# A two-layer transformer with experts: layer 1's first modulation product moved into layer 0's routing, and the split weights' tiles lent to the first experts

## The chip, the cores and the metric

The kernel runs on one core of one Trainium2 chip. The metric is the device time of one execution in microseconds. Before the change it is 1314.4 us, the median of 3 runs (1313.9 to 1314.6). The core has TensorE (PE, and PEld for its weight loads), VectorE (DVE), ScalarE (ACT), GpSimd (POOL) and SyncE (SP); SP is used here to issue the loads of weights, ACT and POOL issue other transfers. A "q" behind an engine's name (SPq) is its queue of transfers.

## What is computed

Two layers of a diffusion transformer work on 256 latent tokens and 256 context tokens of width 1024, in float32. In each layer a vector per stream, silu(c), is multiplied by `w_ada` (1024 x 6144) and gives six modulation vectors. The tokens, scaled and shifted by the first two of these, go through a mixer: differential attention with 4 heads, a depthwise convolution of 31 taps, sigmoid gates and an output projection. A layer norm with residual follows, then a mixture of 16 experts: a router picks 2 experts for each token, each expert is `(silu(h w_gate) * (h w_up)) w_down` with inner width 512, and another layer norm with residual ends the layer. Cut to what matters:

```
mod   = split(silu(c) @ w_ada[l] + b_ada[l], 6)
h     = x * (1 + mod[1]) + mod[0]
x     = layer_norm(ALPHA * x + mod[2] * mixer(h), ln1_g[l], ln1_b[l])
h     = x * (1 + mod[4]) + mod[3]
x     = layer_norm(ALPHA * x + mod[5] * grouped_moe(h), ln2_g[l], ln2_b[l])
```

In the last layer only the latent tokens are carried on.

## The kernel before, in words

**Modulation** (`ada`, L339). The 6144 columns of `w_ada` are done in three groups of 2048. A group takes 8 loads of 1 MB (128 rows each, L347) and, for each load, one group of matmuls: four products with 32 rows of output, side by side on TensorE (L349; the profile shows two records for each product, so 8 for a load). The sum stands in one PSUM bank through all 8 loads. Then the bias is added, which two small transfers on POOL brought (L345), the row is transposed, and two DVE copies write `modT`. `ada` is a generator that yields after each load, so that other code can run it a few loads at a time.

**Weights.** Nearly all weights come through `load_raw` (L240), one SP transfer of 1 MB into a tile of 128 x 2048. The usual tiles are the `raw` ring of 3. Products of many tokens use a three-term split: ACT casts the weights to float32r (`whi`, L258), DVE takes the rest (`wlo`, L259), each into rings of 4 tiles of 128 x 1024, and `mm3` (L289 to L293) multiplies high by high, and high by low twice. Where few tokens meet an expert, `raw` is multiplied directly in float32 (`expert64`, L1235 and L1256; `expert32`, L1281 and L1301).

**Layer 0's mixer** (L465). Weights of blocks of 512 columns are multiplied one after the other, and a hook `fill` (L1533) is called between. Its first ten calls run two loads each of `ada(0, 1)` and `ada(0, 2)`, the other two groups of layer 0; the later calls, from the attention on, run two loads each of `ada(1, 0)`, layer 1's first group. So this product's loads and matmuls lie in layer 0's attention, beside the gates' products. The attention of each head is a chain over TensorE (scores, L625), DVE (maximum, L630), ACT (exponential, L632), DVE, transposes, ACT and TensorE again (L646). After the mixer, six small DVE operations (L1551 to L1553) combine layer 1's `modT` with layer 0's last norm into the scale and shift `gt`, `bt` that layer 1's mixer begins with.

**Output projection and routing.** `out_proj` (L751) multiplies by `w_out`, normalizes, computes the router's logits and writes the modulated tokens to DRAM (`hdr`, L866). `route` (L870) is mostly small DVE operations on 128 partitions, with two short groups on TensorE (L942 and L944, L972). It gives an order of the experts by number of tokens (`rank`, `erow`) and the indices `gidx`, `sidx`, `idx2` of the tokens. POOL then gathers the tokens of the first tasks with indirect transfers (`fetch`, L1107).

**Experts of layer 0.** They run in the order of L132, by rank: 0, 1, 8, 9, 10, 2, 3, ... Ranks 0 and 1 are always experts 14 and 15 (`AHEAD`, L96), so their weights can be asked for before the routing is known; for each later one SP reads the expert's number first (L1404). An expert takes 6 loads of 1 MB. Ranks 0, 1 and 8 to 15 have few tokens and use `raw` weights directly; ranks 2 to 7 split them. `loads` (L1069) is lazy, and the steps of consecutive experts are interleaved (L1412), so the loads come in the order gate, gate, up, up of the first expert, gate, gate, up, up of the second, down, down of the first, and so on. The tiles come from `most_tiles` (L211), which goes round through the 3 `raw` tiles, 4 tiles of its own (`raw2`, named raw in the profile) and the two large tiles `m0a`, `m0b`: 9 in all.

**What sets the order.** The code names the engine of each operation. The order on each engine and queue is made by the framework when the kernel is built, from the order in the code, the dependences and a simulated timeline (L1596); `follow` (L249) adds order edges by hand. On the chip each engine and each queue works through its list strictly in order, and an instruction that waits holds all behind it.

Of the kernel before, what the change touches and what calls it, by code (L numbers as in the profile page):

```python
# [24 lines left out]
F32 = mybir.dt.float32  # L25
F32R = mybir.dt.float32r
# [117 lines left out]
N2 = (4, 3)  # L144
# [7 lines left out]
def dit_kernel(ctx: ExitStack, tc: tile.TileContext, A, out):  # L152
    nc = tc.nc
    V, S, G, PE, SP = nc.vector, nc.scalar, nc.gpsimd, nc.tensor, nc.sync
# [3 lines left out]
    ring = ctx.enter_context(tc.tile_pool(name="ring", bufs=1))  # L158
    pm = ctx.enter_context(tc.tile_pool(name="pm", bufs=1))
# [5 lines left out]
    def bank(tag):  # L165
        pool, cfg = banks["now"]
        return pool.tile([128, 512], F32, name=tag, bufs=cfg[tag])

    class scoped:


        def __init__(self, name, keep=False, **cfg):
            assert sum(cfg.values()) <= 8
            self.sb = tc.tile_pool(name=name, bufs=1, reuse_waits="tile")
            self.ps = None if keep else tc.tile_pool(name=name + "_ps", bufs=1, space=bass.MemoryType.PSUM, reuse_waits="tile")
            self.cfg = cfg
# [23 lines left out]
    def raw_tile():  # L200
        return ring.tile([128, 2048], F32, name="raw", bufs=3)

    def more_tiles(pool):

        while True:
            for i in range(pool[1]):
                if i < 3:
                    yield raw_tile()
                yield own_tile(pool)

    def most_tiles(pool, extra):  # L211

        while True:
            for i in range(pool[1]):
                if i < 3:
                    yield raw_tile()
                yield own_tile(pool)
            for name in ("m0a", "m0b"):
                yield pm.tile([128, 2048], F32, name=name)
            if extra:  # L220
                yield pm.tile([128, 2048], F32, name="m1a")

    def own_tile(pool):
        return pool[0].tile([128, 2048], F32, name="raw2", bufs=pool[1])

    def own_tiles(pool):
        while True:
            yield own_tile(pool)

    raws = {"from": None}  # L230
# [8 lines left out]

    def load_raw(src, pat=None, after=None, **kw):  # L240
        t = next(raws["from"]) if raws["from"] else raw_tile()
        hold["load"] = SP.dma_start(t.rearrange(pat, **kw) if pat else t, src)
        if after is not None or hold["y"] is not None:
            follow(hold["load"], after or hold["y"])
        return t
# [3 lines left out]
    def follow(inst, other):  # L249

        tc.add_manual_dep(getattr(inst, "ins", inst), getattr(other, "ins", other).name, in_order,
                          reason="off the critical path")
        return inst

    hold = {"split": None, "y": None}
# [19 lines left out]
    def block_raws(w3, c0, nk, after=None):  # L275

        return [load_raw(w3[:, k0:k0 + 4, c0:c0 + 512], "p (k n) -> p k n", after, n=512) for k0 in range(0, nk, 4)]
# [17 lines left out]
    def transposed(ps, src, n=128):  # L295
        return PE.transpose(ps, src, ident[:src.shape[0], :src.shape[0]])
# [42 lines left out]
    def ada(l, g, tag):  # L339

        ps = bank(tag)
        bv = bias.rearrange("(j q) n -> j q n", q=32)
        src = A["b_ada"][l, g * 2048:(g + 1) * 2048].rearrange("(j n) -> j n", j=4)
        for i in range(2):
            G.dma_start(bv[:, i, :], src)  # L345
        for k in range(KC):
            raw = load_raw(A["w_ada"][l, k * 128:(k + 1) * 128, g * 2048:(g + 1) * 2048])  # L347
            for j in range(4):
                PE.matmul(ps[32 * j:32 * j + 32, :], cs[:, k, :], raw[:, j * 512:(j + 1) * 512],  # L349
                          start=k == 0, stop=k == KC - 1, tile_position=(0, 32 * j))  # L350
            if k < KC - 1:
                yield
        m = small.tile([128, 512], F32, name="modrow", bufs=1)
        V.tensor_tensor(m, ps, bias, op=OP.add)
        if g == 0:
            ps = bank("tr")
            for c in range(4):
                transposed(ps[:, c * 128:(c + 1) * 128], m[:, c * 128:(c + 1) * 128])
            pv = ps.rearrange("p (c j s) -> p c j s", c=4, j=4)
            V.tensor_copy(modT[l][:, :, 0:2, :], pv[:, :, 0:2, 0:2])  # L360
            V.tensor_scalar(modT[l][:, :, 2:4, :], pv[:, :, 2:4, 0:2], 1.0, None, op0=OP.add)
        else:
            dst = moddr[l][:, g * 2048:(g + 1) * 2048].rearrange("s (j n) -> s j n", j=4)
            mv = m.rearrange("(j q) n -> j q n", q=32)
            for i in range(2):
                G.dma_start(dst[i], mv[:, i, :])
        yield

    def run(steps, n=None):
        while n is None or n > 0:  # L370
            if next(steps, 0) == 0:
                return
            n = None if n is None else n - 1
# [88 lines left out]
    def first_block(l):  # L462
        return block_parts(block_raws(A["w_in"][l].rearrange("(k p) n -> p k n", p=128), U_OFF + CC, KC), (V, V) if l else (G, G))
# [605 lines left out]
    def loads(l, e, rows=False):  # L1069
        for src, n in units(l, e, rows):  # L1070
            yield load_raw(src, "p (k n) -> p k n", n=n)
# [5 lines left out]
    def chunks(raws, n, engs=((V, V), (V, V))):  # L1077
        res = []
        for e in engs:
            for hi, lo in split_unit(next(raws), e):  # L1080
                for j in range(0, 1024, n):
                    res.append((hi[:, j:j + n], lo[:, j:j + n]))
        return res

    def first_gate(l, pre):
        raws["from"] = more_tiles(pre)
        ws = loads(l, DENSE[l], True)
        return ws, chunks(ws, 512, ((V, V), (G, G)))

    def moe(l, lg, mh, ml, xn, early, pre_cm, pre):  # L1090
        last = l == NL - 1
# [22 lines left out]
        def more(tasks):  # L1114

            while len(ahead) < len(tasks):
                ts = tasks[:len(ahead) + 1]
                if sum(t[1] for t in ts if not isinstance(t, int)) > 3 or sum(isinstance(t, int) for t in ts) > 3:
                    return
                ahead.append(fetch(ts[-1]))  # L1120
# [261 lines left out]
        order = expert_order(l)  # L1382
        ahead.append(fetch(order[0]))
        more(order)

        for tt in range(T // 128):
            for h in range(4):
# [2 lines left out]
                hold["x1"] = G.tensor_tensor(xn[tt][:, hs], xn[tt][:, hs], res[1][:, hs], op=OP.add)  # L1390
        if DENSE[l] is not None:
            dense(*early, [([mh[k // 4][:, k % 4, tt] for k in range(KC)], [ml[tt][:, k] for k in range(KC)]) for tt in range(T // 128)])
        raws["from"] = most_tiles(pre, last)
        before = iter(())
        for n, task in enumerate(order):
            more(order[n:])
# [4 lines left out]
            if rk < len(AHEAD[l]):  # L1401
                src = loads(l, AHEAD[l][rk])
            else:
                src = loads(l, SP.value_load(erow[0:1, rk:rk + 1], min_val=0, max_val=NE - 1))  # L1404
            if rk in TINY[l]:
                steps = expert32(src, *xs, TINY[l].index(rk))
            elif isinstance(task, int):
                steps = expert64(src, *xs, FEW[l].index(rk))
            else:
                steps = expert(src, xs, [CAP[l] * rk + i for i in range(task[1])])  # L1410
# [9 lines left out]
        first = None if last else first_block(l + 1)  # L1420
# [85 lines left out]
    for tt in range(4):  # L1506
        src = (A["x"] if tt < 2 else A["ctx"])[0, (tt % 2) * 128:(tt % 2) * 128 + 128, :]
# [14 lines left out]
    def ahead():  # L1522
        yield from ada(0, 1, "po")
        yield from ada(0, 2, "sc")
        scaled_rows(0)

    def later():
        yield from ada(1, 0, "mm")

    steps, calls = ahead(), [0]  # L1530
    steps2 = later()

    def fill():  # L1533
        calls[0] += 1
        t = calls[0]
        if t <= 10:
            run(steps, 2 if t > 1 else 0)
        else:
            run(steps2, 2)

    m = mixer(0, xT, lambda k, s: modT[0][:, k % 4, 2 + k // 4, s:s + 1],
              lambda k, s: modT[0][:, k % 4, k // 4, s:s + 1], fill)
    gt = cst.tile([128, KC, 2], F32, name="gt1")
    bt = cst.tile([128, KC, 2], F32, name="bt1")
    pt0 = prm[0][0]
    for s in range(2):
# [4 lines left out]
        V.tensor_tensor(gv, scv, pt0[:, 13:21].rearrange("p (j c) -> p j c", j=2), op=OP.mult)  # L1551
        V.tensor_tensor(bv, scv, pt0[:, 21:29].rearrange("p (j c) -> p j c", j=2), op=OP.mult)
        V.tensor_tensor(bv, bv, shv, op=OP.add)  # L1553

    def experts(l, m, res_src):
        pre_cm = scoped(f"pre{l}", True)
        pre = (pre_cm.open(), N2[l])
        lg, early, xn = out_proj(l, *m, res_src, lambda: first_gate(l, pre))
        return moe(l, lg, *m[:2], xn, early, pre_cm, pre), xn

    first, x1 = experts(0, m, res0)

    def ahead():
        yield from ada(1, 1, "po")
# [3 lines left out]
    steps = ahead()  # L1568
    ticks = iter((1,) * 4 + (2,) * 6)

    def fill1():
        run(steps, next(ticks, 16))

    m = mixer(1, None, lambda k, s: gt[:, k, s:s + 1], lambda k, s: bt[:, k, s:s + 1], fill1,
              lambda s, pool, modulate: combine(0, s, x1, pool, modulate), first)
    _, x1 = experts(1, m, lambda tt: xres[tt * 128:tt * 128 + 128, :])
# [23 lines left out]
```

## Time and profile before

| what | value |
|---|---|
| median of 3 runs | 1314.4 us (1313.9 to 1314.6) |
| the profiled execution: its time, its span | 1314.02 us, 1312.2 us |
| mean granted TensorE clock over the span | 0.927 of full speed |
| PE busy | 1119.2 us (85%) |
| DVE busy | 757.6 us (58%) |
| ACT busy | 451.9 us (34%) |
| POOL busy | 265.4 us (20%) |
| SP's transfer queue (q1) | 304.11 MB, 60.2% of 16 engines' span |
| HBM read and written over the span | 262 GB/s |

Times in the rows below are microseconds from the start of the span. Busy time is the time in which an engine had an instruction running; matmuls overlap, so a TensorE that is busy all the time need not be at its peak. In the order of time a line gives start, duration, engine, source line, operation, output and inputs, and how many were merged; what stands in brackets is the idle time before it and who ended that. [...]

### The profile page before, as it was taken

Reading aid. Unit: us, or ns where it says so; the run is one execution under the profiler, and the core shown is the slowest. Engines: PE = TensorE matmul, PEld = TensorE weight load, DVE = VectorE, ACT = ScalarE, POOL = GpSimd, SP = SyncE. Lnnn points to the kernel's source line nnn. Section 1 sums busy time; section 2 is a strip of 40 time slices with the busy share of each in tenths; the row PEclk is TensorE's granted clock in tenths of the full one; section 3 lists DMA queues with packets and bytes.
Section 4 is the critical chain, followed back from the end, with each engine's and each line's share of the span. In section 5 each row is a group of like instructions: output and inputs, shape, how many; then the busy total and the mean of one; then the engine's idle time right before and its main releaser. Section 6 shows DMA issues by size and latency. Waiting matters only on the chain. (4 is left out here: it accounts for less than half of the span.)

```text
span 1312.2 us, 18928 instructions
## 1 busy us (share of the span) xinstructions
PE 1119.2 (85%) x7210; PEld 812.7 (62%) x7210; DVE 757.6 (58%) x1290; ACT 451.9 (34%) x759; POOL 265.4 (20%) x410
## 2 busy tenths in 40 slices
PE   4799999998999288998988277999998869998981
PEld 1577666776878154676675156776797555775760
DVE  0638987767376701554745379995668932424355
ACT  1421223435322311454644223323654512313240
POOL 2500010000001593101001250001002781110021
PEclk8799999999999689999998678999999879998996
DMA  8666566111257379988999576565339468899984
GB/s 304 199 223 233 219 231 225 62 65 64 76 201 293 117 299 414 423 346 307 423 424 382 198 273 224 191 241 180 129 121 344 157 241 359 327 397 425 411 344 157
DMA packets 80878, 336.30 MB, mean 256 GB/s; under 512 B 10333, under 2 KB 10637, under 8 KB 52369
## 3 DMA queue, kind: packets, MB, share of 16 engines
q1 hardware_dynamic: 66784, 304.11, 60.2%
q0 software_dynamic: 10080, 19.01, 4.4%
q10 hardware_dynamic: 3920, 11.95, 2.4%
q8 instruction: 58, 0.95, 0.3%
q14 instruction: 36, 0.29, 0.1%
HBM read 327.21 MB, written 16.52 MB: 262 GB/s over the span
## 5 line engine op out<-in xcount | busy, mean ns | idle before, releaser
L259 DVE TENSOR_TENSOR wlo<-raw,whi 128x1024 fp32r<-128x1024 f32 x196 | 237.0, 1226 | 111.2 <-ACT whi L258 109.5
L258 ACT CAST whi<-raw 128x1024 fp32r<-128x1024 f32 x204 | 210.9, 1050 | 209.0 <-PE mm L293 117.5
L681 DVE SCALAR_TENSOR_TENSOR cv<-cv,cwt,cv 128x512 f32<-128x512 f32 (+1 forms) x240 | 135.5, 612 | 0.9
L289 PE MATMUL mm<-hh,whi 128*128 128x512 f32 (+1 forms) x384 | 132.7, 351 | 3.9 <-DVE gt L486 1.8
L292 PE MATMUL mm<-hl,whi 128*128 128x512 f32 (+1 forms) x384 | 131.7, 346 | 2.9 <-DVE hl L489 2.9
L293 PE MATMUL mm<-hh,wlo 128*128 128x512 f32 (+1 forms) x384 | 129.7, 345 | 0.0
L289 PEld LDWEIGHTS mm<-hh,whi 128*128 128x128 f32 x384 | 74.2, 194 | 22.6 <-issue 8.3
L292 PEld LDWEIGHTS mm<-hl,whi 128*128 128x128 f32 x384 | 73.8, 193 | 21.9 <-issue 11.1
L289 PE MATMUL mm<-whi,xt 128*128 128x512 f32 x192 | 77.1, 407 | 6.4 <-ACT whi L258 6.0
L292 PE MATMUL mm<-wlo,xt 128*128 128x512 f32 x192 | 79.2, 413 | 3.6 <-DVE wlo L259 3.5
L293 PEld LDWEIGHTS mm<-hh,wlo 128*128 128x128 f32 x384 | 73.1, 192 | 13.7 <-issue 4.5
L293 PE MATMUL mm<-whi,xt 128*128 128x512 f32 x192 | 77.6, 404 | 0.0
L292 PE MATMUL mm<-wlo,hh 128*128 128x512 f32 x176 | 70.3, 399 | 0.0
L293 PE MATMUL mm<-whi,hl 128*128 128x512 f32 x176 | 69.8, 397 | 0.0
L289 PE MATMUL mm<-whi,hh 128*128 128x512 f32 x176 | 69.6, 405 | 0.0
L1235 PE MATMUL mm<-raw,xt 128*64 128x256 f32 x464 | 56.7, 392 | 0.9 <-DMA raw<-in_w_e_up_dram 0.7
L1242 DVE SCALAR_TENSOR_TENSOR v<-v,mm 128x256 f32<-128x256 f32 x9 | 3.8, 421 | 81.2 <-ACT v L1241 81.2
L307 POOL TENSOR_TENSOR rs<-rs,nhalf 128x1 f32<-128x1 f32 x18 | 14.4, 805 | 174.3 <-DVE rs L306 174.2
L292 PEld LDWEIGHTS mm<-wlo,xt 128*128 128x128 f32 x192 | 37.7, 196 | 16.7 <-DVE wlo L259 6.7
L289 PEld LDWEIGHTS mm<-whi,xt 128*128 128x128 f32 x192 | 37.1, 194 | 17.2 <-ACT whi L258 7.8
L1235 PEld LDWEIGHTS mm<-raw,xt 128*64 128x64 f32 x464 | 33.6, 141 | 21.4 <-issue 4.3
L349 PE MATMUL po<-raw,cs 128*32 128x512 f32 x128 | 20.0, 685 | 29.8 <-DVE al L1463 24.9
(397 smaller groups left out, 2267.4 us busy)
## 6 DMA issues: line engine op xcount, KB each, us to landing
raw<-in_w_ada_dram SPq DMA_DIRECT2D x48, 1024.0 KB, 7.6
raw<-in_w_e_down_dram SPq DMA_DIRECT2D x48, 1024.0 KB, 13.6
raw<-in_w_e_up_dram SPq DMA_DIRECT2D x47, 1024.0 KB, 13.7
raw<-in_w_e_gate_dram SPq DMA_DIRECT2D x44, 1024.0 KB, 13.6
raw<-in_w_in_dram SPq DMA_DIRECT2D x36, 1024.0 KB, 5.0
m0a<-in_w_e_up_dram SPq DMA_DIRECT2D x9, 1024.0 KB, 8.2
raw<-in_w_out_dram SPq DMA_DIRECT2D x8, 1024.0 KB, 5.0
m0b<-in_w_e_gate_dram SPq DMA_DIRECT2D x7, 1024.0 KB, 10.6
```

The lines of the kernel that those rows point to most:

```text
L258: j = S.copy(hi, src)
L259: i = eng.tensor_tensor(lo, src, hi.bitcast(F32), op=OP.subtract)
L289: i = PE.matmul(ps, lhs[0], rhs[0], start=first, stop=False)
L292: PE.matmul(ps, lhs[0], rhs[1], start=False, stop=False)
L293: PE.matmul(ps, lhs[1], rhs[0], start=False, stop=last)
L307: return G.tensor_tensor(dst, dst, nhalf[:, :n], op=OP.pow)
L349: PE.matmul(ps[32 * j:32 * j + 32, :], cs[:, k, :], raw[:, j * 512:(j + 1) * 512], start=k == 0, stop=k == KC - 1, tile_position=(0, 32 * j))
L681: i = V.scalar_tensor_tensor(av, win, cwt[:, cb, j:j + 1], av, op0=OP.mult, op1=OP.add)
L1235: PE.matmul(ps[64 * j:64 * j + 64, u * 256:u * 256 + 256], xt[:, k, k0 // 4, :], raw[:, k * 512 + j * 256:k * 512 + j * 256 + 256], start= ...
L1242: V.scalar_tensor_tensor(v, v, 1.0, ps[:, :256], op0=OP.add, op1=OP.mult)
```

## The change

Three things change. First, `ada(1, 0)` is no longer run by `fill` in layer 0's mixer; it is run as a whole in layer 0's `moe`, after `route` and the first gathers have been written down and before the experts, with the 3 `raw` tiles. Second, the loads of layer 0's experts take their tiles in another order: first the 4 own tiles, then `m0a`, `m0b`, then four pairs of a `whi` and a `wlo` tile (a pair holds the two halves of one load, brought by two transfers of 512 KB), and then the old round of 9. Since the first two experts take 12 loads, in the order given above, the pairs serve the second expert's up weights and the first expert's down weights. Third, the six DVE operations for `gt` and `bt` come after layer 0's experts. Layer 1's experts keep their tiles.

```
+    class Halves:
+        def __init__(self):
+            self.parts = [ring.tile([128, 1024], F32R, name=name, bufs=4).bitcast(F32) for name in ("whi", "wlo")]
+        def __getitem__(self, at):
+            rows, cols = at
+            h = cols.start // 1024
+            assert (cols.stop - 1) // 1024 == h
+            return self.parts[h][rows, cols.start - 1024 * h:cols.stop - 1024 * h]
+
+    def early_tiles(pool):
+        for _ in range(pool[1]):
+            yield own_tile(pool)
+        for name in ("m0a", "m0b"):
+            yield pm.tile([128, 2048], F32, name=name)
+        for _ in range(4):
+            yield Halves()
+        yield from most_tiles(pool, False)
...
     def load_raw(src, pat=None, after=None, **kw):
         t = next(raws["from"]) if raws["from"] else raw_tile()
+        if isinstance(t, Halves):
+            d = src.shape[1] // 2
+            for h, part in enumerate(t.parts):
+                hold["load"] = SP.dma_start(part.rearrange(pat, **kw), src[:, h * d:h * d + d])
+            return t
...
         order = expert_order(l)
         ahead.append(fetch(order[0]))
         more(order)
+        if not last:
+            raws["from"] = None
+            run(ada(1, 0, "mm"))
...
-        raws["from"] = most_tiles(pre, last)
+        raws["from"] = most_tiles(pre, True) if last else early_tiles(pre)
...
-    def later():
-        yield from ada(1, 0, "mm")
     steps, calls = ahead(), [0]
-    steps2 = later()
     def fill():
         calls[0] += 1
         t = calls[0]
-        if t <= 10:
-            run(steps, 2 if t > 1 else 0)
-        else:
-            run(steps2, 2)
+        run(steps, 2 if t > 1 else 0)
...
+    def experts(l, m, res_src):
...
+    first, x1 = experts(0, m, res0)
     gt = cst.tile([128, KC, 2], F32, name="gt1")
     bt = cst.tile([128, KC, 2], F32, name="bt1")
...
         V.tensor_tensor(bv, bv, shv, op=OP.add)
-    def experts(l, m, res_src):
...
-    first, x1 = experts(0, m, res0)
```

## Rows read from the trace of the kernel before

**Rows 1.** Busy time by stretch: length, each engine, PEclk, DMA share, GB/s.

```profile
160.00:240.00 80.00, 80.00 (x392) 51.51 (x391) 64.35 (x102) 24.80 (x51) 8.37 (x13) 1.00 0.60 211
...
430.00:440.00 10.00, 3.38 (x34) 1.95 (x34) 8.08 (x18) 3.03 (x10) 9.69 (x8) 0.78 0.15 60
440.00:450.00 10.00, 0.76 (x9) 0.66 (x8) 8.57 (x47) 4.49 (x6) 0.00 (x0) 0.50 0.51 188
450.00:460.00 10.00, 1.88 (x8) 0.83 (x8) 4.44 (x18) 0.00 (x0) 5.83 (x17) 0.50 0.19 61
```

**Rows 2.** Order of time on TensorE, in the routing of layer 0.

```profile
435.10 0.33 PE L296 MATMUL lg<-cp,lgt 128*128 128x128 f32 x1 [0.44 <-ACT lgt L835]
445.74 0.28 PE L942 MATMUL sc<-oh,upper 128*128 128x144 bf16 x1 [10.31 <-DVE oh L917]
...
450.33 2.03 PE L972 MATMUL sc<-Am,Bm 128*128 128x64 f16 x8 [3.83 <-DVE Bm L971]
463.77 0.49 PE L296 MATMUL tr<-cp,xs 128*128 128x128 f32 x1 [11.41 <-DMA xs<-hdr,idx]
```

**Rows 3.** Busy time by stretch, in the first experts (columns as in rows 1).

```profile
500.00:530.00 30.00, 26.87 (x188) 14.59 (x184) 4.36 (x8) 4.92 (x10) 5.01 (x5) 1.00 1.01 411
530.00:560.00 30.00, 27.84 (x121) 20.32 (x120) 18.11 (x18) 15.44 (x18) 3.63 (x3) 1.00 1.01 421
```

**Rows 4.** Order of time on TensorE, in the first experts.

```profile
522.38 1.95 PE L1235 MATMUL mm<-m0a,xt 128*64 128x256 f32 x16 [1.14 <-DMA m0a<-in_w_e_up_dram]
...
531.97 0.73 PE L289 MATMUL mm<-whi,xt 128*128 128x512 f32 x2 [1.63 <-ACT whi L258]
```

**Rows 5.** Order of time on SP's queue of transfers.

```profile
380.85 0.82 SPq L242 DMA_DIRECT2D raw<-in_w_e_gate_dram  x2
...
424.16 0.33 SPq L242 DMA_DIRECT2D m0b<-in_w_e_down_dram  x1
469.41 0.33 SPq L242 DMA_DIRECT2D raw<-in_w_e_down_dram  x1
```

**Rows 6.** Waits of SP's queue from 420 to 480: total, times, longest.

```profile
SPq L1404 <- DVE erow L988: 29.7, 1, 29.7
```

**Rows 7.** The modulation's line from 180 to 215: its instructions on TensorE.

```profile
L349 PE MATMUL mm<-raw,cs x64: 592/593/617, 183.2 to 213.3; 128*32 128x512 f32 x64
```

**Rows 8.** Order of time on TensorE, in the attention.

```profile
183.15 1.06 PE L349 MATMUL mm<-raw,cs 128*32 128x512 f32 x8
184.15 0.50 PE L289 MATMUL mm<-hh,whi 128*128 128x512 f32 x1
184.48 0.39 PE L292 MATMUL mm<-hl,whi 128*128 128x512 f32 x1
184.71 0.40 PE L293 MATMUL mm<-hh,wlo 128*128 128x512 f32 x1
```

**Rows 9.** Busy time by stretch, in the attention (columns as in rows 1).

```profile
182.00:214.00 32.00, 32.00 (x156) 15.79 (x156) 20.27 (x36) 8.12 (x19) 2.31 (x4) 1.00 0.71 253
214.00:246.00 32.00, 30.95 (x149) 23.79 (x149) 26.94 (x44) 13.42 (x29) 2.66 (x3) 1.00 0.39 132
246.00:278.00 32.00, 31.48 (x141) 22.46 (x142) 20.96 (x35) 11.95 (x27) 0.00 (x0) 1.00 0.20 66
```

**Rows 10.** Transfers by target: count, size of one, median us from issue to landing.

```profile
raw<-in_w_ada_dram SPq DMA_DIRECT2D x48, 1024.0 KB, 7.6
```

**Rows 11.** Busy time by stretch, at the first gathers (columns as in rows 1).

```profile
458.00:461.00 3.00, 0.00 (x0) 0.00 (x0) 0.00 (x0) 0.00 (x0) 2.21 (x3) 0.50 0.78 231
461.00:464.00 3.00, 0.23 (x1) 0.23 (x2) 0.00 (x0) 0.00 (x0) 2.51 (x3) 0.50 0.79 269
...
467.00:470.00 3.00, 3.00 (x18) 1.76 (x16) 0.00 (x0) 0.00 (x0) 3.00 (x5) 0.55 0.02 5
```

**Rows 12.** Order of time on DVE, between the layers.

```profile
746.43 0.75 DVE L1461 SCALAR_TENSOR_TENSOR ah<-ah,gates 128x512 f32<-128x512 f32 x1 [12.11 <-DMA ah<-ydr]
```

More of the change, by code (lines that the diff above doesn't have):

```diff
@@ L1535, in fill @@
         t = calls[0]
-        if t <= 10:
-            run(steps, 2 if t > 1 else 0)
-        else:
-            run(steps2, 2)
+        run(steps, 2 if t > 1 else 0)
     m = mixer(0, xT, lambda k, s: modT[0][:, k % 4, 2 + k // 4, s:s + 1],
               lambda k, s: modT[0][:, k % 4, k // 4, s:s + 1], fill)
+    def experts(l, m, res_src):
+        pre_cm = scoped(f"pre{l}", True)
+        pre = (pre_cm.open(), N2[l])
+        lg, early, xn = out_proj(l, *m, res_src, lambda: first_gate(l, pre))
+        return moe(l, lg, *m[:2], xn, early, pre_cm, pre), xn
+    first, x1 = experts(0, m, res0)
     gt = cst.tile([128, KC, 2], F32, name="gt1")
@@ L1553, in dit_kernel @@
         V.tensor_tensor(bv, bv, shv, op=OP.add)
-    def experts(l, m, res_src):
[L1556 to L1559, printed above, removed]
-    first, x1 = experts(0, m, res0)
     def ahead():
```

## Prediction, made before the changed kernel was run

> **What bounds the kernel now.** I read the busy time by stretch first, then the order in time of the queues in the stretches that the change touches. [...] After the last product of the logits at 435.10 TensorE has nothing but two short groups, at 445.74 and 450.33, until the first expert's transposes at 463.77, which waited 11.41 us for the gathered tokens [rows 2]. That is 28.7 us with some 3 us of work, at the half clock (0.50), and the DMA engines are at 0.15, 0.51 and 0.19 in the three stretches from 430 to 460 [rows 1]. Then the expert weights are the bound: from 500 to 560 the DMA engines are at 1.01, 411 to 421 GB/s, and TensorE is idle for 3.1 + 2.2 = 5.3 us of these 60 [rows 3], as before the products at 522.38 and 531.97 [rows 4]. The chain that ended last doesn't reach back this far, so I don't use it.
>
> Why do the DMA engines rest in the routing? The queue of weight loads (SP) issues expert loads from 380.85 on; the ninth goes out at 424.16, the tenth only at 469.41 [rows 5]. Nine tiles are all there are, and the tenth load needs one that the first expert has read; in between, SP also waits 29.7 us for the expert indices of the routing [rows 6].
>
> **Part 1, the modulation product leaves the attention.** Its records run from 183.2 to 213.3, 64 of them, which is 8 loads by 8 records [rows 7]. The group at 183.15 holds TensorE for 1.00 us up to the product at 184.15, and the product after that comes 0.33 us later, where two products in a row are 0.23 us apart (184.48 to 184.71) [rows 8]: 1.10 us a group, 8 groups, **-8.8 us**. The cover would be gone if the attention's own chain (reduction on DVE, exponential on ACT, transposes) were late next. It speaks against this that DVE is busy 20.3 + 26.9 + 21.0 = 68.2 us in the 96 us from 182 to 278, which still fit into 87, and that from 246 to 278, with the attention running and no modulation product in it, TensorE is still busy 31.5 of 32 us [rows 9]. Ends: 0 (the chain takes it all; a loss is excluded, since work only goes) and -8.8; I take -8.8, by the second of these rows. The 8 loads leave SP's queue there as well; TensorE is busy for all 32 us from 182 to 214 [rows 9], so it isn't short of weights and that is worth nothing, as is the PSUM bank it held. The two bias DMAs, the add and the two copies into the transposed modulation are the same few instructions at another place.
>
> **Part 2, the same product in the routing.** The groups need 8 x 1.06 us at the full clock, some 17 us at half, and fit into the 28.7 us [rows 2, 8]. The bytes need 8 x 2.5 us (a load is 1024 KB, 1.05 MB, at 411 to 421 GB/s [rows 3, 10]). Free from 430 to 460 are 8.5 + 4.9 + 8.1 = 21.5 us [rows 1]: 8 or 9 loads, and there is some room ahead of that, so it fits with little over. But these loads go through the ring of three tiles, and a tile comes back only when TensorE has run its group, in a PSUM bank that the output projection uses until about 424, when its last input tile is free too [rows 5]. Three loads can go out from 381 on, as expert loads do now, and are in by then. The other five are two rounds of 7.6 us from issue to landing [rows 10]: 424 + 15.2 = 439, which is ahead of the routing's own two groups. If the six expert tiles that come free at the same time (two large ones, four of split halves) are served between them, 6 x 2.5 = 15 us later: 454, plus a group at the half clock, 456.4, against 450.33 [rows 2]. So if the planner put the last group in front of the routing's second one, the routing would wait 0 to 6 us. I take 0: the 7.6 us were taken with three of these loads in flight. What is queued behind a late group is the one-hot product, then the indices, the gathers, and the first expert.
>
> The gathers have a second price. The first expert waits for its own [rows 2], and in the 6 us from 458 to 464 the DMA engines are at 0.78 and 0.79 with the gathers alone [rows 11], 4.7 us of transfer. With the three ring tiles free early, loads for the first routed experts will now be in flight then. Ends: 0, and +4.7 us (half the engines' time); I take the middle, **+2.3 us**. [...]
>
> **Part 3, more tiles for the first experts.** They get 4 own tiles, 2 large ones and 4 pairs of halves: 10 loads instead of 9 need no tile to come back. The three ring tiles are behind these in the new order, and free once the modulation product is done, so at least one more load goes out between the indices, which follow the group at 450.33, and the first expert at 463.77 [rows 2]. Two loads more at 2.5 us are **-5.0 us**, and TensorE waits 5.3 us for weights from 500 to 560 [rows 3], so nearly all of it counts; from 560 on it works through large experts and the shift is handed on. Ends: 0 and -5.3. The halves cost two issues of 512 KB instead of one, on a queue that waits rather than works: nothing. The four half tiles of each kind are read by unsplit experts, long before the first split product at 531.97 [rows 4]: nothing.
>
> **Part 4, the scale and shift of layer 1** (six small DVE operations, about 1 us) come after layer 0's experts. DVE sits idle there for 12.11 us until 746.43, waiting for the expert rows [rows 12]: nothing; without that cover 1 us.
>
> Sum: -8.8 + 2.3 - 5.0 = -11.5 us. The profiled execution took 1314.02 us (span 1312.2), which gives 1302.5; the median of the runs is 0.4 above it, so I say **1303 us**.
>
> **Clock.** In the stretch from 467 to 470 the granted clock is still 0.55 [rows 11], although the experts have begun. If groups in the gap kept it high, at most some 3 us of 6 at half speed would come back. I count nothing for it, since a gap up to the gathers stays, and let the low end of the range hold it. [...]
>
> **Rivals.**
> *The routing takes back what the experts gain.* The modulation's last group does stand ahead of the routing's second product and lands late (+6), and the gathers get half the engines (+4.7): -8.8 - 5.0 + 10.7 = -3.1, and with any other slip no change: 1311 to 1315, say 1313. For it: one in-order queue on TensorE and little room on the DMA. Against: the 439 worked out above is ahead of both of the routing's groups. 0.08.
> *The attention's chain is the bound after all*, so the moved product gives nothing back there: -5.0 + 2.3 = -2.7, 1311.5. For it: DVE at 26.9 of 32 us from 214 to 246 [rows 9]. Against: the busy TensorE from 246 on. 0.08, of which 0.05 is faster by the bound.
> *The loads don't fit the gap and land in the weights' stage* (the change doesn't do what it says). If the five loads that need a ring tile back are served only when the experts run, each takes 2.5 us from a full queue [rows 3], and the extra tiles are filled no earlier: -8.8 + 12.5 = +3.7, 1318; all eight would be +11. It decides from four such loads on. For it: SP is one queue in order, and a load that waits for a tile holds all behind it. Against: the 28 us in which nothing else wants TensorE. 0.12, slower.
>
> **How the numbers follow.** The forecast's own case has 0.72, 1297 to 1310: -8.8 - 5.3 - 3 = -17 at the low end, and at the other the 4.7 for the gathers and some loss in part 1 or 3. About 0.2% (2.6 us) is what a measurement of this kernel can tell from no change, so faster means under 1311.8 and slower over 1317. Faster: 0.72 + 0.05 = 0.77; same: 0.08 + 0.03 = 0.11; slower: 0.12. The range that leaves out no more than 2 in 10 runs from 1297 over the two middle rivals to 1315.
>
> **What would show it.** Right: no modulation product between 180 and 215, and everything from the gates on some 9 us earlier up to the logits; eight groups between 424 and 456 (before's time, less 9); DMA above 0.7 from 430 to 460; the first expert's transposes no more than 33 us after the last logits product; idle of TensorE for weights in the first experts near 0. Wrong: gaps on TensorE in the attention that end on DVE or ACT; a wait of the routing's products on modulation loads; modulation groups after the first expert has started; a gather that takes several us more. The prediction falls if the stage up to the logits is not at least 6 us shorter, or if the span from there to the first expert grows by over 8 us.

## The result, and the profile after

The changed kernel takes 1297.6 us (median of 4 runs, 1296.9 to 1299.9), the kernel before 1314.2 beside it: ratio 0.988 [0.985, 0.991], 16.6 us less. The forecast was 1303.0, 11.5 less. The profiled span fell from 1312.2 to 1295.2 us. The lines of the code moved by 27 to 30 places: L349, the modulation product, is L376 now, L1235 is L1262.

What happened to each stage is read from fixed points of the two traces (us; the last column is what the stage from the row above gained or lost):

| point | before | after | stage |
|---|---|---|---|
| first attention scores of layer 0 | 182.1 | 179.8 | -2.3 |
| second token tile's `qt` transposes | 285.6 | 275.3 | -8.0 |
| first product with the conv weights | 303.6 | 298.3 | +5.0 |
| last transpose of the logits | 435.1 | 430.2 | +0.4 |
| first expert's transposes | 463.8 | 462.5 | +3.6 |
| first product of a large expert | 532.0 | 525.7 | -5.0 |
| DVE's combine of layer 0 starts | 746.4 | 734.8 | -5.4 |
| last transpose of layer 1's logits | 1027.0 | 1014.6 | -0.8 |
| layer 1's dense expert: `act` transposes | 1069.7 | 1048.0 | -9.3 |
| last instruction | 1307.6 | 1290.7 | +4.9 |

The -2.3 at the start is no part of the change: the same product starts at 182.0 in a second profile of it, below. First the busy time by stretch of the changed kernel (length, each engine, PEclk, DMA share, GB/s; PEclk is TensorE's granted clock as a share of its full speed, the DMA share the mean over the 16 engines):

```profile
290.00:295.00 5.00, 5.00 (x18) 3.14 (x17) 1.63 (x7) 1.94 (x5) 0.00 (x0) 0.51 0.02 3
295.00:300.00 5.00, 4.18 (x13) 2.19 (x13) 3.01 (x8) 3.98 (x16) 0.00 (x0) 0.50 0.00 0
...
430.00:440.00 10.00, 4.59 (x25) 1.19 (x26) 8.39 (x30) 3.10 (x5) 4.95 (x4) 0.67 1.02 417
440.00:450.00 10.00, 7.83 (x41) 2.22 (x40) 7.05 (x33) 1.77 (x4) 0.00 (x0) 0.50 1.02 416
450.00:460.00 10.00, 4.11 (x20) 0.82 (x20) 3.83 (x18) 0.00 (x0) 7.71 (x19) 0.67 0.73 259
500.00:530.00 30.00, 28.09 (x187) 16.44 (x184) 8.63 (x12) 9.61 (x16) 7.57 (x7) 1.00 1.01 406
530.00:560.00 30.00, 30.00 (x137) 22.83 (x136) 18.81 (x21) 15.80 (x20) 0.00 (x0) 1.00 1.00 414
```

The gap is filled as meant: the DMA share from 430 to 460 is 1.02, 1.02, 0.73 where it was 0.15, 0.51, 0.19 [rows 1], and from 530 to 560 TensorE is busy throughout, before for 27.84 of 30 us [rows 3]. What was not expected are the first two lines: TensorE runs at a granted clock of 0.51 and 0.50 there. The same stretches before:

```profile
290.00:295.00 5.00, 5.00 (x27) 3.52 (x26) 3.55 (x8) 2.55 (x4) 0.00 (x0) 1.00 0.02 6
295.00:300.00 5.00, 3.77 (x27) 2.93 (x26) 3.46 (x12) 2.63 (x11) 0.55 (x1) 1.00 0.62 210
```

The order of time on TensorE in the routing of the changed kernel:

```profile
430.18 0.48 PE L323 MATMUL lg<-cp,lgt 128*128 128x128 f32 x1 [0.93 <-ACT lgt L862]
430.59 4.18 PE L376 MATMUL mm<-raw,cs 128*32 128x512 f32 x24
441.69 0.28 PE L969 MATMUL sc<-oh,upper 128*128 128x144 bf16 x1 [6.91 <-DVE oh L944]
...
442.38 3.64 PE L376 MATMUL mm<-raw,cs 128*32 128x512 f32 x16
446.27 1.52 PE L999 MATMUL sc<-Am,Bm 128*128 128x64 f16 x6 [0.25 <-DVE Bm L998]
447.72 1.94 PE L376 MATMUL mm<-raw,cs 128*32 128x512 f32 x8
449.58 0.29 PE L999 MATMUL sc<-Am,Bm 128*128 128x64 f16 x2
450.56 1.94 PE L376 MATMUL mm<-raw,cs 128*32 128x512 f32 x8 [0.69 <-DMA raw<-in_w_ada_dram]
452.98 1.52 PE L376 MATMUL mm<-raw,cs 128*32 128x512 f32 x8 [0.48 <-DMA raw<-in_w_ada_dram]
...
462.50 1.95 PE L323 MATMUL tr<-cp,xs 128*128 128x128 f32 x8 [6.52 <-DMA xs<-hdr,idx]
```

All eight groups lie between 430 and 455, as worked out, but the planner (the framework's ordering when the kernel is built) put one of them (447.72) between the sixth and the seventh index product. DVE, which makes the indices from these products, shows the delay, first before and then after, and the last gathers of GpSimd show when the first expert's tokens were asked for:

```profile
452.40 0.22 DVE L975 TENSOR_SCALAR gidx<-sc 128x64 int32<-128x64 f32 x1 [0.33 <-PE sc L972]
459.81 1.00 POOL L1107 DMA_INDIRECT xs<-hdr,idx  x1 [0.30 <-issue]
```

```profile
449.91 0.23 DVE L1002 TENSOR_SCALAR gidx<-sc 128x64 int32<-128x64 f32 x1 [1.91 <-PE sc L999]
457.32 1.01 POOL L1134 DMA_INDIRECT xs<-hdr,idx  x1 [0.31 <-issue]
```

So of the 3.6 us that the routing grew, 1.6 are the wait for the index products and 1.2 the gathers (5.2 us from this issue to the first expert's transposes, 4.0 before). Most of the rest lies earlier on DVE, where three small products took 1.36 us beside a GpSimd operation and 0.40 before (the last section has such rows).

The largest single gain, 9.3 us, is in layer 1, whose code is untouched; the end of layer 1 loses 4.9 of it again in this pair of traces. In the kernel before, TensorE's waits from 1040 to 1065 and GpSimd's order of time there:

```profile
PE mm L292 <- POOL wlo L259: 11.7, 1, 11.7
```

```profile
1050.75 1.12 POOL L1107 DMA_INDIRECT xg<-hdr,gidx  x1 [0.16 <-ACT whi L258]
1052.17 1.02 POOL L1107 DMA_INDIRECT xg<-hdr,gidx  x1 [0.30 <-issue]
1053.27 0.72 POOL L1389 TENSOR_TENSOR m1b<-m1b,y 128x256 f32<-128x256 f32 x1
...
1054.31 4.80 POOL L1389 TENSOR_TENSOR m1b<-m1b,y 128x256 f32<-128x256 f32 x7
1059.07 2.34 POOL L259 TENSOR_TENSOR wlo<-raw,whi 128x1024 fp32r<-128x1024 f32 x1
```

The second weight split that GpSimd makes for the dense expert stands behind two gathers and eight multiplications, and TensorE waits 11.7 us for it. In the changed kernel the planner, which orders the whole program, put both splits together, ahead of the index copies, and that wait is gone:

```profile
1028.14 4.66 POOL L286 TENSOR_TENSOR wlo<-raw,whi 128x1024 fp32r<-128x1024 f32 x2 [5.25 <-ACT whi L285]
1035.82 2.23 POOL L1032 COPY both<-gidx 64x1 int32<-64x1 int32 x4 [3.02 <-DVE gidx L1002]
```

### The profile page after: what moved, and what is told of

The parts are those of the page before. It is cut to its first block, busy times and chain, and to the rows that moved or that the text cites. A ratio compares the mean times of both kernels' runs of the same rounds, so it can differ in the third digit from the quotient of the medians.

```text
span 1295.2 us, 18927 instructions
## 1 busy us (share of the span) xinstructions
PE 1130.7 (87%) x7210; PEld 815.9 (63%) x7210; DVE 756.0 (58%) x1290; ACT 451.5 (35%) x759; POOL 268.8 (21%) x410
## 5 line engine op out<-in xcount | busy, mean ns | idle before, releaser
L286 DVE TENSOR_TENSOR wlo<-raw,whi 128x1024 fp32r<-128x1024 f32 x194 | 233.7, 1221 | 92.0 <-ACT whi L285 90.5
L1262 PE MATMUL mm<-raw,xt 128*64 128x256 f32 x448 | 54.5, 396 | 0.9 <-ACT xt L1255 0.9
L393 POOL DMA_DIRECT2D moddr<-modrow x8 | 4.7, 588 | 197.7 <-DVE modrow L381 197.7
L1262 PEld LDWEIGHTS mm<-raw,xt 128*64 128x64 f32 x448 | 32.5, 143 | 20.5 <-issue 4.5
L376 PE MATMUL po<-raw,cs 128*32 128x512 f32 x128 | 20.1, 688 | 27.5 <-DMA raw<-in_w_ada_dram 27.5
L316 PEld LDWEIGHTS mm<-whi,hh 128*128 128x128 f32 x176 | 33.2, 189 | 15.7 <-issue 7.5
```

Of the source, the lines that this page charges most:

```text
L286: i = eng.tensor_tensor(lo, src, hi.bitcast(F32), op=OP.subtract)
L316: i = PE.matmul(ps, lhs[0], rhs[0], start=first, stop=False)
L1262: PE.matmul(ps[64 * j:64 * j + 64, u * 256:u * 256 + 256], xt[:, k, k0 // 4, :], raw[:, k * 512 + j * 256:k * 512 + j * 256 + 256], start= ...
```

## The experiments

Each was timed beside the kernel before, whose medians in the four groups were 1315.8, 1315.0, 1314.5 and 1313.8. The diffs are cut to their core and stand against the changed kernel where nothing else is said; `hold["g"]` is GpSimd's last weight split, `hold["x1m"]` the last of its multiplications.

**The changed kernel again, and each part alone.**

> The changed kernel once more, for a second profile beside the others of this group. Time: about 16 us below before, as measured. What is open is the granted clock: in the first profile of this kernel it fell to 0.51 from 290 to 300 us, where before had 1.00, which took back some 5 us, and the first 80 us were better by 2.3 us. Theory A (the fall belongs to this order of instructions): it falls again within 280 to 305, and the first product with the conv branch's weights starts again at 298 (before 303.6). Rival (an accident of one execution): the clock stays at 1.00 there, and that product starts at 293 or so.

Measured: 1299.1 us, 0.988 [0.985, 0.990]. The clock falls again (0.59 from 290 to 300), and from the first scores to the conv product it is 118.9 us, 118.5 in the first profile, 121.5 before.

```diff
-        raws["from"] = most_tiles(pre, True) if last else early_tiles(pre)
+        raws["from"] = most_tiles(pre, last)
```

> Only the modulation product is moved into the routing; the expert weights keep the old tiles. By the prediction's sum: -8.8 in the attention, +2.3 at the gathers, 6.5 us below before. By the traces of before and after (theory A): -8.0 in the attention, +5.0 from the clock at 290 to 300, +3 in the routing, -5 in layer 1, where the planner puts the second weight split of GpSimd ahead of the index copies here too: 5 us below before, and about 11 above the changed kernel. Rival: the extra tiles pay only while the product stands in the routing or the reverse (the two parts share the freed DMA time, so they don't add): 10 us or more below before.

Measured: 1316.9 us, 1.002 [1.000, 1.004]. No theory written down for this run had it, and the prediction's sum gave 6.5 less: the moved product alone gains nothing, although layer 1's split is early here too. The attention is as in the changed kernel, but the large experts start at 537.6 (before 532.0) and layer 0's experts last 273.9 us from the first transposes to the last count (DVE's `nover`, the number of overflow tiles), 262.9 before and 255.5 in the changed kernel. SP's queue shows why in the first part, up to the large experts: the product's loads hold the ring's three tiles, so that six expert loads and not nine [rows 5] stand ahead of the product's last five, and the others come after them:

```profile
448.25 0.33 SPq L269 DMA_DIRECT2D raw<-in_w_ada_dram  x1
452.74 0.33 SPq L269 DMA_DIRECT2D raw<-in_w_e_gate_dram  x1
456.40 0.33 SPq L269 DMA_DIRECT2D raw<-in_w_e_up_dram  x1
462.80 0.33 SPq L269 DMA_DIRECT2D raw<-in_w_e_gate_dram  x1
474.77 0.33 SPq L269 DMA_DIRECT2D raw<-in_w_e_down_dram  x1
```

For the next one the diff goes the other way: the kernel before, with `Halves`, `early_tiles` and the loads into them, and the product left in the attention.

```diff
-        raws["from"] = most_tiles(pre, last)
+        raws["from"] = most_tiles(pre, True) if last else early_tiles(pre)
```

> Only the idle tiles of the split weights are used for the first experts; the modulation product stays in the attention. By the prediction's sum: 5.0 us below before. Theory A: the same 5 in the first experts, and 5 more in layer 1, whose code is untouched, because the planner orders GpSimd's second weight split ahead there in this kernel as well: 10 us below before, with no wait of TensorE for that split near 1060 us. Rival: the layer 1 gain came from the moved product (its modulation is ready by another time): then 5, and that wait of some 11 us is still there.

Measured: 1305.2 us, 0.992 [0.990, 0.995]: theory A's 10. TensorE's wait near 1060 is gone, so the planner's new order comes with either part.

```diff
             raws["from"] = None
-            run(ada(1, 0, "mm"))
+            V.memset(modT[1], 0.0)
```

> The changed kernel without layer 1's first modulation product: its vector is set to zero, its eight loads and products are left out. It prices the product in the routing. By the prediction: the index group isn't delayed by it, gathers +2.3, so 2.3 us below the changed kernel. Theory A, from the two traces: the stage from the last logits transpose to the first expert grew by 3.6, of it 2.4 ahead of the indices and 1.2 at the gathers, so 3.6 below. Rival: the first experts are bound by weight loads and not by their start, so an earlier start is given back as waits for weights: 0 to 1; or the other way, the 8 loads left out let more expert weights land early: 5 or more.

The time as a whole (1642 us) can't be compared: with a zero vector layer 1 has eight overflow tiles to compute (124.4 us of TensorE in their products of L1367 alone). Up to layer 0's experts the trace holds. From the last logits transpose to the first expert it has 30.7 us; the changed kernel has 32.3 and 31.1 in its two profiles, the kernel before 28.7. So the product is 0.4 to 1.6 us of the growth, and 2.0 are there without it. The gathers take almost as long without the product: 5.0 us from issue to the first expert's transposes, 5.2 and 5.4 with it, 4.0 before.

**Layer 1's order.** In the changed kernel (e4) one dependence puts the second split behind the multiplications. In the kernel before (e5) one puts the multiplications behind the split; to name it, e5 also writes layer 1's multiplications and the additions after them down behind the dense expert.

```diff
+            follow(hold["g"], hold["x1m"])     # e4: split after the last multiplication
```

> The changed kernel with one order forced back: in layer 1, GpSimd's second weight split stands behind the eight x1 multiplies again, as in the kernel before. Theory A (layer 1 gained because the planner put this split ahead of the index copies): the wait of TensorE on that split comes back, some 11 us long in before, and 4 to 5 us of the gain are lost: about 1303. Rival (layer 1 gained by something else, as the clock or the rest of layer 0): no change, 1298.

```diff
+                    follow(i, hold["g"])       # e5: each multiplication after the split
```

> The kernel before, neither part of the change in it, with the reverse order forced: in layer 1 the x1 multiplies of GpSimd stand behind the second weight split. They take 0.72 + 4.80 us there, and the split would end some 5.6 us earlier than 1061.4. Theory A: the dense expert's products start 5 us earlier and the time falls by 4 to 5 us, to about 1310 where before has 1314 to 1316, so that part of what was measured for the change can be had without it. Rival: the x1 rows or another wait are late next, 0 to 1 us.

Measured: 1307.0 us, 0.993 [0.991, 0.996], and 1307.1 us, 0.994 [0.991, 0.996]. TensorE's waits for the split, of the one and the other:

```profile
PE mm L319 <- POOL wlo L286: 11.9, 1, 11.9
```

```profile
PE mm L292 <- POOL wlo L259: 5.9, 1, 5.9
```

Both were larger than expected: 8 to 9 us of the change's gain go with that place (1307.0 against 1297.6 and 1299.1), and the kernel before gets 7.9 us from it without the change. What the change itself brings is the other 8. It isn't the place alone: the planner orders the rest of layer 1 around it, in e4 as in the kernel before, in e5 in a way of its own. By the traces, from the last transpose of layer 1's logits to the last instruction, it is 280.5 us before, 282.5 in e4, 276.1 and 277.5 in the changed kernel, 269.6 in e5, so the traces put 5.0 to 6.4 us on it where the medians of e4 and the changed kernel put 8 to 9.

With layer 1's split early in all four, the parts can be set side by side:

| | nine tiles, as before | ten and the ring |
|---|---|---|
| product in the attention | 1307.1 (e5) | 1305.2 (e2) |
| product in the routing | 1316.9 (e1) | 1297.6, 1299.1 (e0) |

Moved alone the product costs 9.8 us; the tiles alone bring 1.9, which is not clear of the runs' noise; together they bring 8 to 9.5. Layer 1's order isn't the same in the four, e5's least, so here is the same up to the last transpose of layer 1's logits, from the first attention scores: 844.9 us before, 841.5 with the tiles alone, 856.1 with the product alone, 834.8 and 837.0 with both. Alone the product costs 11, the tiles bring 3.4, and together they bring 7.9 to 10.1: the two parts don't add.

**How many tiles.**

```diff
-        for _ in range(4):
+        for _ in range(2):
             yield Halves()
```

> The changed kernel with two tiles of split halves instead of four for the first experts, so eight of their loads can go out ahead of the first expert instead of ten; the product stays in the routing, and the planner keeps layer 1's early split. Without the extra tiles (the product alone, 1316.9) the kernel was 18 us above the changed one, where the prediction had 5.0 for them. Theory A (two loads of 2.5 us that land in the weight-bound stretch): the first large expert starts 5 us later, seen as waits for weights between 460 and 560, and the time is 1303. Rival 1 (the tiles are worth more than their loads, because the stage also loses the clock in its waits): 1307 or more. Rival 2 (the loss without the tiles lies in the order of the later experts): about 1298, or a loss that begins only after 560 us.

Measured: 1311.0 us, 0.999 [0.997, 1.001], 12 to 13 above the changed kernel: rival 1's size, and most of it where rival 2 looks. The first large product comes at 528.0, 2.3 us later; the other 9 are lost after 600. SP's waits from 560 to 730 for the small experts' down products, and the busy time from 590 to 640, of before, of e1, of this kernel and of the changed one:

```profile
SPq L242 <- PE sc L1256: 2.8, 1, 2.8
590.00:640.00 50.00, 44.18 (x334) 31.91 (x331) 25.82 (x30) 24.11 (x35) 6.05 (x6) 0.97 0.87 341
```

```profile
SPq L269 <- PE sc L1283: 18.1, 3, 9.4
590.00:640.00 50.00, 43.73 (x338) 31.13 (x337) 26.06 (x29) 23.96 (x33) 5.71 (x5) 0.97 0.71 268
```

```profile
SPq L269 <- PE sc L1283: 11.1, 1, 11.1
590.00:640.00 50.00, 45.89 (x299) 33.52 (x299) 29.42 (x32) 27.71 (x37) 5.58 (x5) 0.93 0.81 317
```

```profile
SPq L269 <- PE sc L1283: 5.1, 1, 5.1
590.00:640.00 50.00, 46.66 (x278) 34.26 (x277) 30.27 (x32) 26.82 (x36) 5.43 (x5) 0.93 0.89 361
```

In these traces a load waits for the tile whose turn it is, and no load goes out meanwhile: here the queue waits 11.1 us up to 624.26, and then eight loads go out in 4.4 us. The number of tiles shifts which load falls on a tile that a small expert's last product still reads. Where one does, all loads behind it stand still, 18.1 us in e1, with 0.16 of 50 us less DMA than before, 8 us, about what that kernel lost after 537 (7.3). TensorE then waits 4.41 us at 655.91 here, for a tile of the next expert. The order of the later experts differs too between these kernels, and the two aren't separated, so for the loss after 600 the tile whose turn it is stays the likely cause and not a shown one.

**The routing.**

```diff
+                    follow(i, hold["index"])   # the product's groups k = 5 to 7
```

> The changed kernel with the last three of the product's eight groups held behind the routing's index products on TensorE. In the traces of the changed kernel DVE waited 1.91 and 0.94 us for the index products, against 0.33 in before. Theory A: indices, gathers and the first expert come 0.6 to 1.6 us earlier, and the kernel with them: 1 us below 1298. Rival: the last modulation tiles come free later, and what is loaded behind them is late by as much: no change, or 1 us slower.

Measured: 1299.7 us, 0.989 [0.987, 0.991]. DVE's wait for the index products is 0.30 us again, and the span from the logits to the first expert 30.8 us, 0.3 to 1.5 less, but the time is that of e0: the rival, no change.

```diff
+                    follow(hold["fetch"], first_xs)        # e7: xg gathers after the first xs
+                    follow(hold["fetch"], last_xs)         # e9: the first three after all three xs
```

> The changed kernel with layer 0's gather for the first expert issued ahead of the three for the larger experts, 3 x 1.3 us that it stands behind now. Theory A (the routing's chain sets the start of the experts, and the ten loaded tiles then feed them): the first expert starts 3.7 us earlier and the kernel ends 3 to 4 us earlier, 1294. Rival (from 470 us on the DMA engines are full, 1.01, so the weights set the end of the stage): the earlier start is given back as waits for weights before 560 us, 0 to 1 us.

> The changed kernel with all three gathers for the small experts ahead of the three for the larger ones in layer 0 (one of them ahead gave a first expert 5 us earlier, but another order of the later experts and the late weight split in layer 1). Here the planner keeps the early split in layer 1. Theory A (the first expert's start is worth its 4 to 5 us when layer 1's order is held): the stage up to the first experts' end is 4 us shorter and the kernel ends at 1294. Rival (the order of the later experts, which differs from the changed kernel's here too, decides): the experts take as much longer as they start earlier, 1298 to 1305.

Measured: 1314.3 us, 1.000 [0.998, 1.001], and 1297.1 us, 0.988 [0.985, 0.990]. In e7 the first expert starts at 457.5, 5 us earlier, and layer 0's experts last 268.8 us instead of 255.5; the late split is back in layer 1 as well. In e9 it starts at 455.9 with only 0.46 us of wait left for the gather:

```profile
454.32 1.11 PE L323 MATMUL tr<-cp,modrow 128*128 128x128 f32 x4 [0.81 <-DVE modrow L381]
455.89 1.10 PE L323 MATMUL tr<-cp,xs 128*128 128x128 f32 x4 [0.46 <-DMA xs<-hdr,idx]
```

From the logits to the first expert that is 27.1 us, 4.0 to 5.3 less, but to the experts' last count only 1.3 to 2.3 less (285.5 against 286.8 and 287.8), and to DVE's combine 1.0 to 1.8 more: all of it is given back. The order of the later experts differs here too. The runs (1293.5 to 1304.0) don't tell e9 from the changed kernel.

**The clock in the attention.**

```diff
+                cb == 0 and tt == 0 and not last and PE.matmul(ps[:, :256], ident, cp[:, :256], start=True, stop=True)
```

> The changed kernel with one product more on TensorE, 256 columns of constants into a bank that the next transposes overwrite, in the patch of small instructions of layer 0's mixer just ahead of where the granted clock falls in every profile without the modulation product in the attention (0.50 from 290 or 292 to 302 us). The order of all other instructions stays. Just before the fall TensorE waits 1.4 us there for DVE; in the kernel before 0.7. Theory A (the idle time in this patch is what lets the clock fall): the product takes some 0.45 us of it, the clock stays at 1.00, and the first product with the conv branch's weights starts 4 to 5 us earlier: 1294. Rival 1 (so little doesn't decide, or the idle time is not the cause): the clock falls as before, and the time is 1298 to 1299.

```diff
-            V.bn_stats(st, ps)
+            st_i = V.bn_stats(st, ps); last or tt != 3 or follow(st_i, heads[12])
```

> The changed kernel with one instruction of DVE moved: the normalization statistics of the conv branch's last token tile stand behind a later attention head, so that the head that TensorE waits for before the clock falls (1.4 us) is not delayed by them. The order of the experts and of layer 1 stays as in the changed kernel. Theory A (that idle time lets the clock fall): the wait is 0.7 as in the kernel before, the clock stays at 1.00 from 285 to 305, and the time is 1294 or so, unless the later statistics make the conv branch late in their turn. Rival: the clock falls all the same, at this place or a little later, and the time is 1297 to 1300.

Measured: 1299.4 us, 0.988 [0.986, 0.991], and 1299.2 us, 0.988 [0.986, 0.990]: the rivals. In e8 the clock falls as before (0.50 from 295 to 300) and TensorE still waits 1.50 us at 290.91. In e10 that wait is 0.72, the clock holds 1.00 to 295 and falls then, around a new wait of 3.75 us for `qt` at 298.46. The one profile without the fall is e9's, whose mixer has the changed kernel's order:

```profile
290.00:295.00 5.00, 3.93 (x24) 2.76 (x24) 3.68 (x11) 2.65 (x7) 1.09 (x2) 1.00 0.27 102
295.00:300.00 5.00, 3.96 (x16) 2.14 (x14) 3.58 (x10) 4.46 (x17) 0.58 (x1) 1.00 0.00 0
```

It has 115.3 us from the first scores to the conv product, where the ten others with the product out of the attention have 118.5 to 123.6. With the product in the attention there are three profiles: before and e2 keep the full clock, but e5, whose layer 0 has the code of the kernel before, falls for some 3 us:

```profile
300.00:302.00 2.00, 2.00 (x11) 1.88 (x10) 1.10 (x4) 1.36 (x4) 0.00 (x0) 0.50 0.00 0
```

So the long fall goes with the moved product in ten profiles of eleven, costs some 3.5 us by the one profile without it, and isn't fixed by TensorE's order; a short one came without the moved product too. What decides it stays open.

## Why the prediction was right, and where it was not

The direction, the range and the mechanism of the gap hold. But half of the 16.6 us are none of its terms, so that the time lies near the forecast is in part luck: without layer 1's order the change brings 8.0 (e4), less than the 11.5. And by its own words it fell: the stage up to the logits was to be at least 6 us shorter, and it is 2.6 us shorter (-8.0, +5.0, +0.4).

- **Part 1, -8.8.** The work leaves nearly as priced: -8.0 up to 275 us, and no wait of DVE's chain took its place; the rival of the attention's chain is out. The step that failed is "nothing else is exposed": without the product the granted clock falls to 0.50 a hundred us later, and some 3.5 of the 5.0 us that come back there are its (115.3 against 118.5 and more, from the one profile that kept the clock). In that profile the stretch still takes 1.8 us more than before: TensorE is idle for 3.75 us in it, 3.26 before, and busy for 1.3 us more, which no run explains. Up to the logits that profile is 6.1 us shorter than before. The clock was considered for the routing alone. The fall comes in a patch of small products with waits (TensorE busy for 4.18 of the 5 us from 295, at 0.50), but the same order has also kept the full clock (e9, 3.96 of the 5 us, at 1.00).
- **Part 2, index 0.** One group stands between the index products and delays them by 1.6 us (0.6 in the second profile). Holding it back changed no time, so the 0 was right for the end though not for the place.
- **Part 2, gathers +2.3.** Measured +1.2 and +1.5, +1.0 without the product and +1.2 with the tiles alone (e2): it comes with the tiles' loads, with or without the product. In the changed kernel the DMA engines are at 1.00 from 458 to 461, before at 0.78 [rows 11]. Half the engines, 4.7, was the author's estimate from the gathers' own two stretches and didn't come about.
- **Part 3, -5.0.** -5.0 up to the first large expert: right. The failed step is that the terms were added. Tiles alone bring 1.9, the product alone costs 9.8, because the product takes the three ring tiles of the expert loads. That is near the third rival's 1318 (e1, 1316.9), but not by its way: the product's last load went out at 448.25, ahead of the first expert, and it is three expert loads that came late instead. Up to the first large expert e1 loses 3.6 us to before by that, and 7.3 more behind it, where the cause isn't separated. The split tiles keep it away: with two of the four pairs 12 us are lost (e11). The experts as a whole last 7.4 us less, 2.5 of it behind the first large expert, for which the sum had no term.
- **Part 4, 0.** Right, but not by the cover that it counted on, DVE's wait before the combine [rows 12]. The planner didn't put the six operations there: they run in the routing, right after the modulation, while DVE has nothing else to do before the gathered tokens arrive:

```profile
456.31 0.17 DVE L1581 TENSOR_TENSOR gt<-modT,pt 128x8 f32<-128x8 f32 x1
```

- **Not in the sum.** The planner's order in layer 1, 8 us. The prediction costed the edit where it stands; the planner orders the program as a whole, and several of the kernels that differ early got another order late (e7 has the late split again).

Own parts 8 (e4 against before) and layer 1's order 8 to 9 make the 16.6.

## What to carry to other kernels

Where a planner orders the program, compare the order of each engine after the edit over the whole kernel first, and time the edit with the changed places pinned back, one at a time: here half the gain came with one instruction's place and the order around it, to be had without the edit. Two parts that use the same ring of tiles are costed together, by what stands ahead of what in the load queue. In e9 an earlier start of the experts, 4.0 to 5.3 us from the logits on, was all given back.

## What the runs showed of the hardware

Four DVE operations of 128x4 took 0.62 us in all before, and 3.19 us in e2, where GpSimd's multiplications and additions of 128x512 ran beside them. The first line is of before, the others are of e2:

```profile
440.73 0.62 DVE L910 SCALAR_TENSOR_TENSOR kg<-gs,mg,cp 128x4 f32<-128x4 f32 x4
```

```profile
437.56 2.60 POOL L888 TENSOR_TENSOR ha<-m1b,sc 128x512 f32<-128x512 f32 x2 [2.93 <-DVE p L911]
440.12 2.48 POOL L889 TENSOR_TENSOR ha<-ha,sh 128x512 f32<-128x512 f32 x2
```

```profile
439.56 3.19 DVE L937 SCALAR_TENSOR_TENSOR kg<-gs,mg,cp 128x4 f32<-128x4 f32 x4
```

The four of e2 run from 439.56 to 442.75, GpSimd's operations in these rows from 437.56 to 442.60. In the changed kernel other small DVE operations last longer: three of `pr` take 1.36 us there, 0.40 before. One of them takes 1.15 us and ends at 435.9, where GpSimd's two additions (from 433.40, 2.50 us) end as well, and the other two take 0.18 us each. Why they last longer is not shown. By these rows, as an estimate, where the planner puts GpSimd's 128x512 operations beside the routing is worth one to two and a half microseconds (1.36 against 0.40, 3.19 against 0.62). Up to the indices e2's routing is 1.3 us longer than before, and not 2.6, since the kernel before lost 1.5 us a little earlier (three operations on the logits' bias, L839, 2.85 us beside GpSimd as well, 1.37 in e2); the gathers add 1.2.

The second surprise is the clock: with the same order of instructions on TensorE a stretch of some 12 us from about 290 had a granted clock of 0.50 in eight profiles and of 1.00 in one.

In these traces what stands later in an engine's or a queue's order ran later at three places where that cost time: GpSimd's second split (1059.07 before) ran behind eight multiplications while TensorE waited 11.7 us for it; in the changed kernel the seventh index product ran behind a group of the modulation (447.72, 1.94 us) and DVE waited 1.91 us; and in e11 eight loads went out only after one that waited 11.1 us.
